# A ConvFFN in seven products per step: sums that grow in PSUM banks, and the low parts of weights on VectorE

## The chip, the cores and the metric

The kernel runs on one core of a Trainium2 chip. Its engines are TensorE (PE; PEld in the profile is its weight load), VectorE (DVE), ScalarE (ACT), GpSimd (POOL) and SyncE (SP), whose queue starts the DMA transfers spoken of here. The metric is the device time of one execution in microseconds, the median of several runs. Lower is better.

## The reference

Two layers act on 1024 latent tokens and 256 context tokens of width 1024, in float32. Layer 0 mixes tokens with a Fourier transform and a spatial gate, layer 1 with neighbourhood attention; each then has a ConvFFN, and this is what the change touches. Layer 0 runs it over latent and context tokens, layer 1 over the latent ones alone.

```
def conv_ffn(h, w_up, conv_w, conv_b, w_down):          # h: tokens x 1024, w_up: 1024 x 5632
    L = h.shape[1]
    a = h @ w_up
    gate, val = a[..., :D_FF], a[..., D_FF:]            # D_FF = 2816
    gp = jnp.pad(gate, ((0, 0), (CONV_W // 2, CONV_W // 2), (0, 0)))
    g = gp[:, 0:L] * conv_w[0] + gp[:, 1:1 + L] * conv_w[1] + gp[:, 2:2 + L] * conv_w[2] + conv_b
    return (jax.nn.silu(g) * val) @ w_down              # w_down: 2816 x 1024
    ...
    x = x + g2 * conv_ffn(modulate(x, norm2_g[layer], sh2, sc2), ffn_w_up[layer], ...)
```

## The kernel before

**Steps.** Features lie on partitions, tokens on columns. The tokens of a layer are worked in two halves, and each half runs 22 steps f = 0 to 21; a step makes the gate features and the value features of one block of 128. So a layer has 44 steps and the kernel 88. A step's product of a 1024 x 256 weight block (A) with the half's tokens (B) is cut into 2 x 2 blocks and made with seven products in place of eight (Strassen's scheme in Winograd's form): P1 = A00 B00, P2 = A01 B10, P3 = S4 B11, P4 = A11 N4, P5 = S1 T1, P6 = S2 T2, P7 = S3 T3. S1 to S4 are sums of weight blocks, T1 to N4 sums of token blocks. The columns of one product are 320 and 324 in layer 0's halves, 256 and 258 in layer 1's.

**Hi and low.** Every operand is split into a rounded part (hi) and the rest (low). `split` makes the hi as a copy on ScalarE (L447) and the low as a subtraction (L448) on VectorE or GpSimd. A product is then 4 blocks of rows x 3 passes (hi hi, hi low, low hi) = 12 matmuls (L306), 84 a step.

**Sums of a step.** ScalarE copies P1's bank into SBUF (L323). Seven VectorE adds (L311) bring in the six other products: c10 = P6 + c00, c00 += P2, c01 = P5 + c10, c10 += P7, c11 = c10 + P5, c10 += P4, c01 += P3. Then the gate: a scaled copy on ScalarE (L315), two shifted multiply-adds on VectorE for the convolution of width 3 (L317, L319), Silu on ScalarE, the product with the value half (L361), and a hi and a low of the result, `act`.

**Down.** `act` of two steps feeds `down` (L376): a step from f = 2 to 20 runs four of its output blocks (48 matmuls; 24 of 512 columns where a half has 512 tokens, layer 1's first). VectorE adds each result from PSUM into the running stream `xl` (L382). AFTER says behind which products the four stand. PSUM has eight banks under the name `pq`, taken in turn by products and `down`.

**Weights.** Each step also makes ready the operands of the next ones. Two DMAs of 512 KB on SP's queue (L236) bring the raw weights into `wr`: load0 brings A00 and A01, load1 brings A10 and A11. `wr` has two buffers, so load0 waits until the buffer that held the last A00 and A01 has been read, load1 until that of A10 and A11 has. GpSimd makes four raw sums: S1 = A10 + A11 (L241), S3 = A00 - A10 in A10's place (L247), S2 = S1 - A00 in A00's place (L248), S4 = A01 - S2 (L251). Seven splits follow. The seven hi and low pairs have one slot each: A00 and S2 side by side in one `wh` tile, S1 and S4 in another, A01, S3 and A11 in a `wq` tile each. The splits of a step are for the step after it, so a slot can be rewritten when this step's product has read it. The `down` weights come by a third DMA (`wrd`) and are split into `wd`.

**Who makes the lows.** With POOL = ("A00", "A01", "A11"), these three lows are made on GpSimd in steps that run `down`; the four others, those of `wd` and of `act` are VectorE's.

**What sets the order.** ORDER is the order of products from f = 1 on: P1, P2, P6, P5, P7, P4, P3. FEED says behind which product each piece of weight work is written. The written order is then rearranged by a scheduler that simulates the engines; the sums, the gate and the split of `act` have high priority. Every engine runs its own list in order, so an instruction that waits holds up all that stand behind it on that engine.

## Time and profile before

| | |
|---|---|
| median of 3 runs | 2914.47 us (2912.04 to 2919.38) |
| profiled execution | 2920.99 us, span 2919.1 us |
| PE busy | 2772.8 us, 95% |
| DVE busy | 2216.9 us, 76% |
| ACT busy | 1302.0 us, 45% |
| POOL busy | 1267.9 us, 43% |

Busy time is a sum over the span; the rest of an engine's time it waits. A group of instructions is shown by line, engine, operation, tiles (out<-in), shapes and count, then its busy time in us and the mean of one in ns, then the idle time of the engine just before them and what ended it. In a timeline a row is start, duration (both us), engine, line, operation, and in brackets the idle time before it. The rows themselves stand in the prediction.

### The profile page before, as it was taken

The numbers are of one execution on the slowest core, as the hardware profiler recorded it, in microseconds if no ns is written. First come the engines' busy times: TensorE is split into PE (matmuls) and PEld (weight loads), VectorE is DVE, ScalarE is ACT, GpSimd is POOL, SyncE is SP. The second block draws the span as 40 slices with busy tenths as digits, with TensorE's granted clock in tenths as the row PEclk, the third lists the DMA queues.
The fourth block names the chain that finished last, engine by engine and source line by source line (L and its number), as shares of the span: only waits on it lengthen the run. The fifth ranks groups of instructions, "written<-read, shape, count | busy, mean of one in ns | idle before, by whom it ended". The sixth has DMA issues, their size and how long they took to land.

```text
span 2919.1 us, 47590 instructions
## 1 busy us (share of the span) xinstructions
PE 2772.8 (95%) x17978; PEld 2522.4 (86%) x17978; DVE 2216.9 (76%) x3748; ACT 1302.0 (45%) x2448; POOL 1267.9 (43%) x1044
## 2 busy tenths in 40 slices
PE   7999998899999999999999998999989999899998
PEld 4668877799999899999888888998778888799998
DVE  4243477999989999998767668996498777887786
ACT  4221314434444443443443336996354444444443
POOL 0600025455555755553311112443455665666663
PEclk9999999899999999999899999999989999999999
DMA  8663262322223222222052327772133323333323
GB/s 303 215 189 118 98 217 72 112 74 86 80 87 101 75 80 87 73 81 87 24 169 101 137 109 183 180 179 80 37 109 101 95 87 98 105 89 93 94 88 95
DMA packets 335886, 327.67 MB, mean 112 GB/s; under 512 B 16217, under 2 KB 264617, under 8 KB 335657
## 3 DMA queue, kind: packets, MB, share of 16 engines
q1 hardware_dynamic: 331509, 315.69, 35.9%
q0 software_dynamic: 3808, 7.87, 0.9%
q8 instruction: 143, 2.34, 0.3%
q10 hardware_dynamic: 340, 1.06, 0.1%
q14 instruction: 86, 0.70, 0.1%
HBM read 277.86 MB, written 46.71 MB: 111 GB/s over the span
## 4 chain that ended last, share of the span: by engine, by line
PE 61%; DVE 14%; DMA 7%; POOL 7%; issue 5%; ACT 5%; SPq 0%; POOLq 0%; DVEq 0%; ACTq 0%
PE pq L306 18%; PE pq L478 15%; PE pq L376 11%; PE ps L478 6%; DMA wr<-in_ffn_w_up_dram 4%; POOL ws L241 2%; DVE xl L382 2%; DVE wh L448 2%; PE pq L566 2%; POOL wh L448 2%; DVE hx L311 2%; PE ps L487 2%; ACT t L1227 1%; POOL wr L248 1%; DMA wd<-in_ada_w_dram 1%
## 5 line engine op out<-in xcount | busy, mean ns | idle before, releaser
L376 PE MATMUL pq<-act,wd 128*128 128x320 f32 (+3 forms) x3696 | 639.8, 322 | 59.3 <-DVE xl L382 24.5
L376 PEld LDWEIGHTS pq<-act,wd 128*128 128x128 f32 x3696 | 557.1, 193 | 92.0 <-DVE xl L382 28.7
L306 PE MATMUL pq<-hs,wh 128*128 128x320 f32 (+3 forms) x4128 | 607.5, 299 | 16.3 <-DVE xl L382 7.8
L306 PEld LDWEIGHTS pq<-hs,wh 128*128 128x128 f32 x4128 | 576.9, 191 | 26.4 <-DVE xl L382 11.2
L306 PE MATMUL pq<-hs,wq 128*128 128x320 f32 (+3 forms) x3144 | 469.8, 299 | 8.4 <-DVE wq L448 4.9
L478 PE MATMUL pq<-hs,wh 128*128 128x512 f32 (+3 forms) x2100 | 469.0, 358 | 3.6 <-DVE hs L724 1.9
L306 PEld LDWEIGHTS pq<-hs,wq 128*128 128x128 f32 x3144 | 442.5, 191 | 14.1 <-DVE wq L448 5.7
L478 PEld LDWEIGHTS pq<-hs,wh 128*128 128x128 f32 x2100 | 365.8, 193 | 78.0 <-issue 6.2
L241 POOL TENSOR_TENSOR ws<-wr 128x512 f32<-128x512 f32 x88 | 153.6, 1745 | 397.3 <-DMA wr<-in_ffn_w_up_dram 333.0
L447 ACT ACTIVATE wh<-wr 128x512 fp32r<-128x512 f32 (+1 forms) x223 | 161.8, 726 | 354.0 <-POOL wr L248 201.5
L382 DVE SCALAR_TENSOR_TENSOR xl<-pq,mod,xl 128x320 f32<-128x320 f32 (+5 forms) x616 | 304.1, 514 | 11.7 <-PE pq L376 11.6
L448 DVE TENSOR_TENSOR wh<-wr,wh 128x512 fp32r<-128x512 f32 (+1 forms) x147 | 166.9, 1135 | 184.8 <-ACT wh L447 184.5
L448 POOL TENSOR_TENSOR wq<-wr,wq 128x512 fp32r<-128x512 f32 x152 | 235.7, 1550 | 32.9 <-ACT wq L447 32.9
L478 PE MATMUL ps<-hs,wh 128*128 128x512 f32 x840 | 240.0, 405 | 3.6 <-ACT hs L721 1.8
L311 DVE TENSOR_TENSOR hx<-hx,pq 128x320 f32<-128x320 f32 (+3 forms) x440 | 196.1, 448 | 29.1 <-PE pq L306 21.6
L447 ACT ACTIVATE wq<-wr 128x512 fp32r<-128x512 f32 x262 | 160.0, 623 | 101.3 <-PE pq L306 73.2
L447 ACT ACTIVATE wh<-ws 128x512 fp32r<-128x512 f32 x172 | 107.5, 625 | 169.8 <-PE pq L306 115.4
L478 PEld LDWEIGHTS ps<-hs,wh 128*128 128x128 f32 x840 | 141.9, 191 | 41.6 <-issue 14.4
L251 POOL TENSOR_TENSOR ws<-wr 128x512 f32<-128x512 f32 x88 | 120.2, 1366 | 123.3 <-DVE wh L448 112.3
L999 POOL TENSOR_TENSOR hsp<-hsq,hsp 128x512 fp32r<-128x512 f32 (+1 forms) x40 | 47.1, 1185 | 265.5 <-ACT hsq L998 265.5
L1006 DVE RECIPROCAL hsq<-hsq 128x512 f32<-128x512 f32 (+1 forms) x40 | 121.1, 3030 | 52.9 <-ACT hsq L1005 52.1
L448 DVE TENSOR_TENSOR wd<-wrd,wd 128x512 fp32r<-128x512 f32 x176 | 155.5, 912 | 0.2 <-ACT wd L447 0.2
(310 smaller groups left out, 4555.5 us busy)
## 6 DMA issues: line engine op xcount, KB each, us to landing
wr<-in_ffn_w_up_dram SPq DMA_DIRECT2D x176, 512.0 KB, 4.4
wrd<-in_ffn_w_down_dram SPq DMA_DIRECT2D x88, 512.0 KB, 3.5
adaw<-in_ada_w_dram SPq DMA_DIRECT2D x128, 256.0 KB, 3.6
wd<-in_ada_w_dram SPq DMA_DIRECT2D x32, 512.0 KB, 5.1
wr<-in_odd_w_qkv_dram SPq DMA_DIRECT2D x24, 512.0 KB, 3.9
vd<-kvs SPq DMA_DIRECT2D x8, 1280.0 KB
v<-vd SPq DMA_DIRECT2D x16, 640.0 KB
kd<-kvs SPq DMA_DIRECT2D x8, 1280.0 KB, 4.6
```

The source lines that it names most:

```text
L241: op(raw["S1"], raw["A10"], raw["A11"], ALU.add)
L251: op(x, raw["A01"], raw["S2"], ALU.subtract)
L306: nc.tensor.matmul(o, w[wn][:, wp, k], self.part(s, bn, k, sp), start=(k == 0 and i == 0), stop=(k == 3 and i == 2))
L311: nc.vector.tensor_tensor(o, x, y, ALU.add)
L376: nc.tensor.matmul(pd, self.wds[j][i][:, wp, d % 4], self.acts[f][:, sp, lo:lo + m], start=(i == 0 and pi == 0), stop=(i == len(fs) - 1 an ...
L382: nc.vector.scalar_tensor_tensor(x, pd[:, a - lo:b - lo], net.mod[:, self.layer, st, 5, d:d + 1], x, ALU.mult, ALU.add)
L447: self.nc.scalar.activation(h, src, AF.Copy)
L448: return (e or self.nc.vector).tensor_tensor(l, src, f32(h), ALU.subtract)
L478: nc.tensor.matmul(o, w(wp, k), s(k, sp), start=(ki == 0 and pi == 0), stop=(ki == len(order) - 1 and pi == 2))
L487: nc.tensor.matmul(out, l[a], r[b], start=(first and i == 0), stop=(last and i == 2))
L566: nc.tensor.matmul(acc[32 * q:32 * q + 32, 0:256], self.sT[:, k, :], w[q // 2][:, 256 * (q % 2):256 * (q % 2) + 256], start=(k == 0), stop ...
L1006: nc.vector.reciprocal(r, r)
```

## The change

For f = 0 nothing changes in the sums. For f > 0, P6 is accumulated in PSUM onto the bank that holds P1, P7 onto P6's, P3 onto P5's, and in steps f = 3 to 20 P4 onto P7's. After each link ScalarE copies the bank's state into SBUF, as far as it is needed there: c00 after P1, c01 after P6, c10 after P7, and c10 again after P4. The adds fall from seven to three (to four at f = 1, 2 and 21, where P4 keeps its own bank and add); the copies rise from one to four (to three). Summed over the four halves, 324 adds go and 240 copies come. A product that continues in a bank must wait until the copy has been read from it.

All lows are made on VectorE: the 228 of A00, A01 and A11 that GpSimd made move there. One `down` of a step stands behind P7 instead of P5. No line of the weight loads or raw sums is edited; their places in each engine's list move with the scheduler. (Lines L311 to L382 of before are L313 to L401 after; L447 and L448 are L466 and L467, L323 is L325.)

```diff
--- before.py
+++ after.py
@@ -92,14 +92,14 @@
 
     ORDER = ("P1", "P2", "P6", "P5", "P7", "P4", "P3")
     FEED = dict(P2=("A00",), P6=("A01",), P5=("S2",), P7=("S1", "load0"), P4=("S3", "A11", "load1"), P3=("S4", "s"))
-    AFTER = dict(P5=1, P4=1, P3=2)
+    AFTER = dict(P7=1, P4=1, P3=2)
     AFTER2 = dict(P4=1, P3=3)
 
     ORDER0 = ("P1", "P2", "P3", "P5", "P6", "P7", "P4")
     FEED0 = dict(P1=("A00",), P2=("A01",), P5=("S1",), P6=("S2", "load0"), P7=("S3",), P4=("A11", "load1", "S4", "s"))
     FEED1 = dict(P6=("A00", "A01"), P5=("S2",), P7=("S1", "load0"), P4=("S3", "A11", "load1"), P3=("S4", "s"))
     BESIDE = {1: (1, 3, 6), 2: (1, 2, 4, 5, 6), 3: (1, 2, 4, 5, 6)}
-    POOL = ("A00", "A01", "A11")
+    POOL = ()
 
     def __init__(self, net, layer, xs, slabs, pool):
         self.net, self.nc, self.layer, self.xs, self.slabs, self.pool = net, net.nc, layer, xs, slabs, pool
@@ -299,12 +299,14 @@
         g = self.t([P, self.w2], "g", bufs=1)[:, :2 * n]
 
         def product(p):
+
             wn, bn = self.PROD[p]
-            o = net.t(net.ps, [P, 512], "pq" if p in ("P2", "P5") else "pq")[:, :n]
+            o = net.t(net.ps, [P, 512], "pq")[:, :n] if p not in onto else x[onto[p]]
             for k in range(4):
                 for i, (wp, sp) in enumerate(PASSES):
-                    nc.tensor.matmul(o, w[wn][:, wp, k], self.part(s, bn, k, sp), start=(k == 0 and i == 0),
-                                     stop=(k == 3 and i == 2))
+                    nc.tensor.matmul(o, w[wn][:, wp, k], self.part(s, bn, k, sp),
+                                     start=(p not in onto and k == 0 and i == 0),
+                                     stop=(k == 3 and i == 2), skip_group_check=p in onto)
             return o
 
         def add(o, x, y):
@@ -319,16 +321,33 @@
                 nc.vector.scalar_tensor_tensor(g[:, c:c + m - 1], C0[:, c + 1:c + m], w2, g[:, c:c + m - 1],
                                                ALU.mult, ALU.add)
             nc.scalar.activation(g, g, AF.Silu)
-        x = {}
-        todo = [("P1", lambda: nc.scalar.activation(c00, x["P1"], AF.Copy)),
-                ("P1 P6", lambda: add(c10, x["P6"], c00)),
-                ("P6 P2", lambda: add(c00, c00, x["P2"])),
-                ("P6 P5", lambda: add(c01, x["P5"], c10)),
-                ("P6 P5 P7", lambda: add(c10, c10, x["P7"])),
-                ("P6 P5 P7", lambda: add(c11, c10, x["P5"])),
-                ("P6 P5 P7 P4", lambda: add(c10, c10, x["P4"])),
-                ("P6 P5 P3", lambda: add(c01, c01, x["P3"])),
-                ("P6 P5 P3 P2", gate)]
+        def copy(o, x):
+            nc.scalar.activation(o, x, AF.Copy)
+        x, onto = {}, {}
+        last = f > 2 and len(downs) > 0
+        if f == 0:
+            todo = [("P1", lambda: copy(c00, x["P1"])),
+                    ("P1 P6", lambda: add(c10, x["P6"], c00)),
+                    ("P6 P2", lambda: add(c00, c00, x["P2"])),
+                    ("P6 P5", lambda: add(c01, x["P5"], c10)),
+                    ("P6 P5 P7", lambda: add(c10, c10, x["P7"])),
+                    ("P6 P5 P7", lambda: add(c11, c10, x["P5"])),
+                    ("P6 P5 P7 P4", lambda: add(c10, c10, x["P4"])),
+                    ("P6 P5 P3", lambda: add(c01, c01, x["P3"])),
+                    ("P6 P5 P3 P2", gate)]
+        else:
+
+            onto = dict(P6="P1", P7="P6", P3="P5")
+            if last:
+                onto["P4"] = "P7"
+            todo = [("P1", lambda: copy(c00, x["P1"])),
+                    ("P2", lambda: add(c00, c00, x["P2"])),
+                    ("P6", lambda: copy(c01, x["P6"])),
+                    ("P7", lambda: copy(c10, x["P7"])),
+                    ("P7", lambda: add(c11, c10, x["P5"])),
+                    ("P4", lambda: copy(c10, x["P4"]) if last else add(c10, c10, x["P4"])),
+                    ("P3", lambda: add(c01, c01, x["P3"])),
+                    ("P3", gate)]
         order, feed = (self.ORDER if f else self.ORDER0, self.FEED if f >= 2 - s else (self.FEED0, self.FEED1)[f])
         cut = 3 - f if f < 2 and s == 0 else 7
         for i, p in enumerate(order):
```

**GpSimd, layer 0's first half, one step.** The tiles are `ws` and `wr` (raw), `wh` and `wq` (the hi and low pairs); the number behind a name is the buffer's. Before:

```order
L241 TENSOR_TENSOR ws_958_7242<-wr_952_7184 128x512
L247 TENSOR_TENSOR wr_952_7184<-wr_948_7147,wr_952_7184 128x512
L448 TENSOR_TENSOR wh_596_3834<-wr_948_7147,wh_596_3834 128x512
L448 TENSOR_TENSOR wq_589_3809<-wr_948_7147,wq_589_3809 128x512
L248 TENSOR_TENSOR wr_948_7147<-ws_958_7242,wr_948_7147 128x512
L251 TENSOR_TENSOR ws_958_7242<-wr_948_7147 128x512
L448 TENSOR_TENSOR wq_608_4158<-wr_952_7184,wq_608_4158 128x512
L241 TENSOR_TENSOR ws_982_7452<-wr_976_7394 128x512
```

And with the change:

```order
L241 TENSOR_TENSOR ws_944_7584<-wr_939_7527 128x512
L247 TENSOR_TENSOR wr_939_7527<-wr_936_7491,wr_939_7527 128x512
L248 TENSOR_TENSOR wr_936_7491<-ws_944_7584,wr_936_7491 128x512
L251 TENSOR_TENSOR ws_944_7584<-wr_936_7491 128x512
L241 TENSOR_TENSOR ws_964_7789<-wr_959_7732 128x512
```

The three lows (L448) are gone from between the raw sums; the four sums keep their order.

**ScalarE, layer 0's first half, an even step.** `g` is the gate (L323 here is its Silu), `hx` takes the copies. Before, from the copy of P1 (L323) over the hi of A01, `act`, S1, S2, S3 and A11 to that of S4:

```order
L323 ACTIVATE hx_840_6198<-pq_842_6200 128x320
L447 ACTIVATE wq_589_3809<-wr_828_6097 128x512
L447 ACTIVATE act_839_6194<-g_817_5989 128x640
L447 ACTIVATE wh_597_3835<-ws_838_6192 128x512
L447 ACTIVATE wh_596_3834<-wr_828_6097 128x512
L447 ACTIVATE wq_590_3810<-wr_832_6134 128x512
L447 ACTIVATE wq_608_4158<-wr_832_6134 128x512
L447 ACTIVATE wh_597_3835<-ws_838_6192 128x512
```

With the change:

```order
L466 ACTIVATE wq_589_3809<-wr_756_5646 128x512
L466 ACTIVATE wh_597_3835<-ws_764_5739 128x512
L323 ACTIVATE g_747_5541<-g_747_5541 128x640
L466 ACTIVATE wh_596_3834<-wr_756_5646 128x512
L325 ACTIVATE hx_766_5745<-pq_768_5747 128x320
L466 ACTIVATE act_765_5741<-g_747_5541 128x640
L466 ACTIVATE wq_590_3810<-wr_759_5682 128x512
L325 ACTIVATE hx_766_5745<-pq_768_5747 128x320
```

These begin with A01, S1, the Silu and S2 (`wh` from `wr`). Behind S2 now stands the copy of P6 (the first L325), and behind the hi of `act` and S3 that of P7, both from bank `pq_768`, which held P1 before and will hold P4.

**ScalarE, layer 1's first half.** Before, over the end of a step, where `wr_3222` holds A10 (then S3) and A11, `wr_3219` A00 (then S2), and `wr_3239` the next A00:

```order
L447 ACTIVATE wh_3041_20746<-wr_3219_22436 128x512
L447 ACTIVATE wh_3042_20747<-ws_3226_22502 128x512
L447 ACTIVATE wq_3025_20649<-wr_3222_22464 128x512
L447 ACTIVATE wq_3048_20973<-wr_3222_22464 128x512
L447 ACTIVATE wh_3042_20747<-ws_3226_22502 128x512
L315 ACTIVATE g_3229_22509<-hx_3228_22508,cols1_31_139,cols4_175_786 128x512
L447 ACTIVATE wd_3253_22726<-wrd_3235_22560 128x512
L447 ACTIVATE wd_3254_22729<-wrd_3235_22560 128x512
L447 ACTIVATE wh_3041_20746<-wr_3239_22608 128x512
```

With the change, where `wr_2999` holds A11 and `wr_3013` the next A00:

```order
L466 ACTIVATE wd_3024_22145<-wrd_3010_21984 128x512
L466 ACTIVATE wd_3025_22148<-wrd_3010_21984 128x512
L466 ACTIVATE wh_2879_20542<-wr_3013_22029 128x512
L325 ACTIVATE hx_3020_22099<-pq_3022_22101 128x256
L466 ACTIVATE wq_2886_20769<-wr_2999_21889 128x512
L325 ACTIVATE hx_3004_21932<-pq_3006_21934 128x256
L466 ACTIVATE wh_2880_20543<-ws_3002_21926 128x512
L317 ACTIVATE g_3005_21933<-hx_3004_21932,cols1_31_139,cols4_175_786 128x512
```

The hi of A11 (`wq` from `wr_2999`) stood before the next load's A00; it now stands behind it (`wh` from `wr_3013`).

## The prediction

> **What bounds the kernel now.** I read the page's busy line and its slices first, then a table of four stretches that hold the steady ConvFFN steps (layer 0 first and second half, layer 1 first and second half), then the chain of waits, then single steps.
>
> ```profile
> PE 2772.8 (95%) x17978; PEld 2522.4 (86%) x17978; DVE 2216.9 (76%) x3748; ACT 1302.0 (45%) x2448; POOL 1267.9 (43%) x1044
> ```
>
> TensorE is busy for 95% of 2919.1 us, so at most 146 us are to be had, wherever they lie.
>
> ```profile
> core 0: us, PE busy (x) PEld busy (x) DVE busy (x) ACT busy (x) POOL busy (x), PEclk, DMA share, GB/s
> 639.00:911.00 272.00, 272.00 (x1852) 271.83 (x1851) 248.54 (x435) 112.82 (x183) 152.40 (x98) 1.00 0.27 82
> 1030.70:1366.30 335.60, 335.22 (x2247) 332.69 (x2246) 305.75 (x532) 137.99 (x223) 183.10 (x119) 1.00 0.27 81
> 2151.20:2500.00 348.80, 324.93 (x2149) 296.68 (x2149) 278.51 (x437) 155.87 (x277) 211.17 (x145) 0.97 0.33 98
> 2594.50:2879.00 284.50, 263.54 (x2114) 261.06 (x2113) 215.03 (x403) 117.97 (x210) 182.20 (x112) 0.98 0.30 89
> ```
>
> GpSimd runs seven weight operations a step, so 98, 119 and 112 operations are 14, 17 and 16 steps: 272.0/14 = 19.43 us a step, 335.6/17 = 19.74, and 284.5/16 = 17.78 in the last stretch. In layer 0 PE is busy throughout; in layer 1 it stands still for 24 and 21 us. What PE alone needs is in the chain of waits (start, us, engine, tile, line, count):
>
> ```profile
> 254.57 5.57 PE ps L478 x24
> 642.48 7.05 PE pq L306 x48
> 1030.71 7.14 PE pq L306 x48
> 2204.84 5.69 PE pq L306 x48
> 2752.82 5.79 PE pq L306 x48
> ```
>
> A matmul takes 7.05/48 = 146.9 ns (320 columns), 148.8 (324), 118.5 (256), 120.6 (258), 232 (512). A step has 84 matmuls of products and 48 of `down` (24 of 512 columns in layer 1's first half): 132 x 146.9 = 19.39, 132 x 148.8 = 19.64, 84 x 118.5 + 24 x 232 = 15.52, 132 x 120.6 = 15.92. So layer 0 is bound by PE to 0.1 us a step, whatever VectorE does. Layer 1 is bound by something else; its period in the first half is read from the load at the head of each step:
>
> ```profile
> 2410.41 4.83 DMA wr<-in_ffn_w_up_dram
> 2427.54 4.83 DMA wr<-in_ffn_w_up_dram
> ...
> 2478.28 4.75 DMA wr<-in_ffn_w_up_dram
> ```
>
> Four steps from 2410.41 to 2478.28: 16.97 us each. What bounds there is in GpSimd's timeline of a step of the second half (start, us, last bracket the idle time before it and who ended it):
>
> ```profile
> 2650.28 2.88 POOL L241 TENSOR_TENSOR ws<-wr 128x512 f32<-128x512 f32 x1 [5.67 <-DVE g L319]
> 2653.24 1.63 POOL L247 TENSOR_TENSOR wr<-wr,wr 128x512 f32<-128x512 f32 x1
> 2654.83 1.73 POOL L448 TENSOR_TENSOR wh<-wr,wh 128x512 fp32r<-128x512 f32 x1
> 2656.53 1.28 POOL L448 TENSOR_TENSOR wq<-wr,wq 128x512 fp32r<-128x512 f32 x1
> 2657.77 1.28 POOL L248 TENSOR_TENSOR wr<-ws,wr 128x512 f32<-128x512 f32 x1
> 2659.13 1.27 POOL L251 TENSOR_TENSOR ws<-wr 128x512 f32<-128x512 f32 x1
> 2660.84 1.29 POOL L448 TENSOR_TENSOR wq<-wr,wq 128x512 fp32r<-128x512 f32 x1 [0.44 <-ACT wq L447]
> 2668.02 3.10 POOL L241 TENSOR_TENSOR ws<-wr 128x512 f32<-128x512 f32 x1 [5.90 <-DMA wr<-in_ffn_w_up_dram]
> ```
>
> It is a closed loop: seven operations, then the second load of raw weights, which may start only when the A11 low (the last L448) has read its buffer, and 17.74 us later the next L241. In it the S2 hi comes late, and VectorE, which runs in order, waits for it:
>
> ```profile
> 2659.75 1.20 DVE L448 TENSOR_TENSOR wh<-wr,wh 128x512 fp32r<-128x512 f32 x1 [4.33 <-ACT wh L447]
> 2661.40 3.15 PE L376 MATMUL pq<-act,wd 128*128 128x258 f32 x24 [1.95 <-DVE xl L382]
> ```
>
> Behind that S2 low stand the `xl` adds that empty PSUM, and PE stops 1.95 us for a bank.
>
> **The change part by part.** *Adds and copies.* 324 adds go (none at f=0, three a step at f=1, 2, 21, four in the 18 others, in four halves) and 240 copies on ScalarE come (two or three a step).
>
> ```profile
> L311 DVE TENSOR_TENSOR hx<-hx,pq 128x258 f32<-128x258 f32 x80 | 33.1, 414 | 1.1
> L323 ACT ACTIVATE hx<-pq 128x258 f32<-128x258 f32 x16 | 5.8, 365 | 0.0
> L448 DVE TENSOR_TENSOR wq<-wr,wq 128x512 fp32r<-128x512 f32 x16 | 11.2, 702 | 0.0
> L447 ACT ACTIVATE wq<-wr 128x512 fp32r<-128x512 f32 x48 | 28.0, 616 | 0.0
> ```
>
> By these rows of the same window of layer 1's second half, a steady step loses 4 x 0.41 = 1.66 us of VectorE and gains 3 x 0.70 = 2.11 of it for the lows, and 3 x 0.365 = 1.10 on ScalarE. Layer 1's VectorE goes from 215.0/16 = 13.4 us a step to about 13.9, under PE's 15.9, and layer 0's from 17.8 to some 18, under 19.4: neither engine sets an end by its total. PE's count does not change; that one `down` stands behind P7, not P5, only enters the counts of matmuls below. So the 324 adds are worth nothing in themselves; PE covers them.
>
> *A wait is added.* P6 may not write P1's bank before ScalarE's copy has left it, P7 not before P6's copy, P4 not before P7's. Nothing in this trace continues a bank after a copy, so bounds: nothing where ScalarE is free (P2's 12 matmuls, 12 x 120.6 = 1.45 us, cover a copy of 0.365), up to a whole hi and a copy where ScalarE stands in its order before another instruction.
>
> *Lows off GpSimd, layer 1's second half.* Out of the loop go 1.73 and 1.28, and the A11 low falls from 1.29 to 0.70. Then the loop is shorter than PE's step. What is left: P4 of an odd step frees A11's slot, and before the next step's first `down` with the newest `act` come A11 hi 0.62, low 0.70, the load 4.15 (alone, quoted below) to 4.83, L241 1.35 (its value in layer 0, below; the 2.88 here is read beside VectorE's two-input operations), S1 hi 0.62, and behind it on ScalarE the hi of that `act`, about as long: 8.06 to 8.74. One engine's next instruction follows 0.08 us after (2653.16 to 2653.24 above); I take 0.1 for each of seven handovers: 8.8 to 9.4. PE has 75 matmuls there (counted in its new order), 75 x 120.6 = 9.05 us. So 0 to 0.4 us of stall every second step, and PE's own 15.92; with a little `xl` waiting left I take 16.3. (17.78 - 16.3) x 18 = 27 us gained; bounds 33 (15.92 and nothing) and 19 (16.7).
>
> *Layer 1's first half.* In the order of the changed kernel ScalarE takes the hi of the next A00, which waits for the first load, before the hi of A11, which frees the buffer of the second. The two loads, side by side before, then stand one behind the other in one loop: L241 1.35 to 1.42, L247 1.53 to 1.63, L248 1.28, S2 hi 0.62 and low 1.20, load 4.15, A00 hi 0.62, copy 0.365, A11 hi 0.62 and low 0.70, load 4.15 to 4.83: 16.6 to 17.4, some handovers lying in the loads' times already.
>
> ```profile
> 521.64 4.15 DMA wr<-in_ffn_w_up_dram
> 2415.37 1.42 POOL L241 TENSOR_TENSOR ws<-wr 128x512 f32<-128x512 f32 x1 [4.99 <-DMA wr<-in_ffn_w_up_dram]
> ```
>
> Against 16.97 now: nothing, give or take 0.3 a step, 5 us in 18. The stall of the old loop goes, and the serial loads take its place.
>
> *Layer 0.* PE leaves nothing to gain, so only a loss is possible. GpSimd's seven become four, the DMAs stay (on SP some loads stand a place earlier or later):
>
> ```profile
> L248 POOL TENSOR_TENSOR wr<-ws,wr 128x512 f32<-128x512 f32 x14 | 24.5, 1750 | 0.0
> L247 POOL TENSOR_TENSOR wr<-wr,wr 128x512 f32<-128x512 f32 x14 | 21.4, 1528 | 1.1
> L241 POOL TENSOR_TENSOR ws<-wr 128x512 f32<-128x512 f32 x14 | 18.8, 1345 | 62.1 <-DMA wr<-in_ffn_w_up_dram 44.9 <-DVE g L317 17.2
> L447 ACT ACTIVATE wq<-wr 128x512 fp32r<-128x512 f32 x42 | 26.4, 629 | 24.0 <-PE pq L306 23.9
> L323 ACT ACTIVATE hx<-pq 128x320 f32<-128x320 f32 x14 | 5.8, 417 | 0.0
> 733.17 1.29 POOL L448 TENSOR_TENSOR wq<-wr,wq 128x512 fp32r<-128x512 f32 x1 [1.06 <-ACT wq L447]
> ...
> 739.19 1.47 POOL L241 TENSOR_TENSOR ws<-wr 128x512 f32<-128x512 f32 x1 [4.74 <-DMA wr<-in_ffn_w_up_dram]
> ```
>
> In its new order ScalarE has the S2 hi (for the next step) ahead of the copy of P6, and P7 waits for that copy. From the end of P4 in an odd step: A11 hi 0.63, low 0.70, load and issue 4.73 (733.17 + 1.29 to 739.19), L241 1.35, L247 1.53, L248 1.28 (as in layer 1's second half) to 1.75, S2 hi 0.63, copy 0.42: 11.3 to 11.7, with up to four handovers 11.4 to 12.1. PE has 71 matmuls between that P4 and P7, 71 x 146.9 = 10.43. So P7 is 1.0 to 1.7 us late in 9 even steps: 12 us lost. In odd steps PE has 101 matmuls there, 14.84 us: no loss. In the second half of layer 0 it has 78 x 148.8 = 11.6: 0 to 0.5 in 9 steps, 2 us lost.
>
> *First steps.* Around 520 to 600 us VectorE itself is full:
>
> ```profile
> 520.00:600.00 80.00, 71.98 (x448) 68.80 (x447) 76.95 (x126) 37.82 (x66) 37.97 (x25) 0.96 0.37 108
> ```
>
> PE idles 8 us beside 96% of VectorE. Only in step 1 of each half do adds go and no low comes (GpSimd took lows only once `down` runs): 3 x 0.48 (layer 0's L311) x 4 = 5.8 us, if VectorE sets the pace; I take half, 3 us gained, bounds 0 and 5.8.
>
> **Sum.** -27 + 0 + 12 + 2 - 3 = -16 us. The profiled execution took 2920.99 us (span 2919.1 and 1.9 around it), 6.5 over the median; 2905 by it, and 2914.47 - 16, about 2898, by the median.
>
> **The rivals.** *PE bounds both layers (0.13).* If ScalarE is early enough everywhere, layer 0 loses nothing and layer 1's first half falls to 15.52 too: 1.45 x 18 = 26, with 33 for the second half and 3 at the start: -62, 2852. For it: VectorE and ScalarE have room. Against: ScalarE's order is fixed, and has the next A00 before A11.
>
> *GpSimd stays slow (slower, 0.18).* L241 takes 2.9 us in layer 1's second half and 1.35 elsewhere; VectorE now runs 0.5 us more of two-input operations a step beside it. If the four raw sums cost the middle of both, 2.1, wherever a chain above has L241 in it, 0.8 us more goes to each: layer 0 loses 19 + 9, layer 1's first half 14, the second half gains 19, the start 3: +20, 2934. It decides from a mean of L241 of about 1.8 us. For it: the row of 2.88 stands beside L448 on VectorE. Against: in layer 0 VectorE is busier, 248.54/14 = 17.8 us a step, and L241 takes 1345 ns.
>
> The Trainium skill, page SBUF — State Buffer, section Who interferes with whom, says that a VectorE operation with two inputs in SBUF and a reading GpSimd operation exclude each other entirely. Fully blocked, the S2 low at 2659.75 would have taken about 0.70 + 0.65, the rest of the L251 beside it, 1.35; it took 1.20, so this trace is near the rule. By it the three lows cost the raw sums as much as before, and the rival above is the one it favours.
>
> *Gains and losses cancel (0.19).* Layer 1's second half at 16.7 (19 gained), its first half at its bad bound (5 lost), layer 0 and the start as summed: -19 + 5 + 14 - 3 = -3, 2911; with nothing gained at the start 2914.
>
> **How the numbers follow.** Forecast 0.50: 2898, its own range 2885 to 2911. This kernel's runs tell about 0.3%, 9 us, from no change, so faster is below 2906, slower above 2923. The forecast puts some 0.39 below 2906, the rest in between with the cancelling case; with the first rival 0.52 faster, 0.27 same, 0.21 slower. Eight in ten: from inside the first rival, 2862, to the slower one, 2934.
>
> **What would show it.** Layer 1's second half at 16.0 to 16.5 us a step, and no PE wait of 2 us on `xl` there. Layer 1's first half still near 17.0, with the two loads end to end. In layer 0, every second step, PE idle of 1 to 1.7 us before P7, ended by ScalarE's copy; PE busy 272.0 of 272.0 there would refute it. L241 near 1.35 in all four stretches; at 2 us or more the second rival holds. Wrong altogether, if layer 0's steps grow by more than 2 us or shrink at all.

## The result: slower by 2.6%, where a small gain was forecast

The changed kernel takes 2989.02 us (median of 4 runs, 2987.93 to 2994.47) against 2914.39 us for the kernel before: a ratio of 1.0258, 95% interval 1.0239 to 1.0276. It is 75 us slower, where 16 us faster was forecast, and far above the forecast's own range of 2885 to 2911. The profiled execution has a span of 2986.1 us, 67.0 more than before.

The page's busy line of the changed kernel:

```profile
PE 2792.4 (94%) x17978; PEld 2532.2 (85%) x17978; DVE 2277.7 (76%) x3652; ACT 1378.4 (46%) x2688; POOL 905.9 (30%) x816
```

The counts say that the change does what it says: 240 more instructions on ScalarE (2448 to 2688), 228 fewer on GpSimd (1044 to 816), 96 fewer on VectorE (324 adds less, 228 lows more). No engine is fuller than before by a share that matters. PE's idle time grew by 47.4 us (146.3 to 193.7). Its busy time for the same 17978 matmuls grew by the other 19.6, at a granted clock of 0.970 over the whole execution in place of 0.974; why, was not looked into. Most of the loss is waiting, as PE's groups of the `down` and product matmuls show (the last fields are PE's idle time before them and what ended it):

```profile
L395 PE MATMUL pq<-act,wd 128*128 128x320 f32 (+3 forms) x3696 | 636.4, 322 | 84.7 <-ACT act L466 55.3 <-DVE act L467 25.1 <-DVE hx L313 2.5
L307 PE MATMUL pq<-hs,wh 128*128 128x320 f32 (+3 forms) x4128 | 621.0, 300 | 16.5 <-DVE hx L313 4.2 <-ACT hx L325 4.0 <-ACT hs L466 3.4
L307 PE MATMUL pq<-hs,wq 128*128 128x320 f32 (+3 forms) x3144 | 483.1, 301 | 35.0 <-ACT hx L325 29.8 <-ACT wq L466 2.1 <-DVE hs L467 1.4
```

PE waits 80 us for `act` (55.3 for its hi, 25.1 for its low) and 34 us for copies out of linked banks (L325). The same groups of the kernel before:

```profile
L376 PE MATMUL pq<-act,wd 128*128 128x320 f32 (+3 forms) x3696 | 639.8, 322 | 59.3 <-DVE xl L382 24.5 <-ACT act L447 21.0 <-DVE hx L311 10.0
L306 PE MATMUL pq<-hs,wh 128*128 128x320 f32 (+3 forms) x4128 | 607.5, 299 | 16.3 <-DVE xl L382 7.8 <-ACT wh L447 4.9 <-DVE wh L448 2.6
```

There `act` stood for 21.0 us by its hi (and 2.6 by its low), the `xl` adds for 32.3, and copies of a linked bank did not exist.

Where in the program: the table takes the start of the hi of `act` (once a step) as the mark. It compares the profiled executions of before, of the change, and of four experiments told below, in us.

| stretch | before | changed | lows alone | down behind P5 | P4's own bank | S hi on GpSimd |
|---|---|---|---|---|---|---|
| layer 0, first half, f = 3 to 20 | 328.8 | 343.9 | 323.6 | 344.6 | 335.6 | 336.5 |
| layer 0, second half | 332.9 | 345.0 | 330.8 | 344.5 | 339.3 | 338.9 |
| layer 1, first half | 286.9 | 305.8 | 279.8 | 303.6 | 276.8 | 296.7 |
| layer 1, second half | 297.5 | 294.8 | 290.5 | 291.6 | 287.4 | 289.9 |
| f = 0 to 3, four halves | 196.3 | 216.4 | 205.6 | 213.5 | 212.3 | 209.5 |
| f = 20 to 21, four halves | 73.1 | 78.3 | 68.6 | 78.3 | 69.5 | 74.8 |

From before to changed: +15.1, +12.1, +18.9, -2.7, +20.1 and +5.2, together 68.7, of 67.0 in the span. A mark moves against PE's work from kernel to kernel: between the same two marks stand, by kernel, up to some 90 matmuls more or less, and 7 matmuls are about 1 us. So a row can tell 10 us too much or too little. PE's idle time between the marks does not count that work:

| PE idle in | before | changed | lows alone |
|---|---|---|---|
| layer 0, first half, f = 3 to 20 | 2.2 | 13.7 | 0.0 |
| layer 0, second half | 0.4 | 10.5 | 0.0 |
| layer 1, first half | 15.8 | 28.1 | 12.9 |
| layer 1, second half | 21.6 | 19.6 | 12.2 |
| f = 0 to 3, four halves | 21.8 | 29.2 | 19.5 |
| f = 20 to 21, four halves | 8.0 | 19.7 | 8.3 |

Windows of the same lengths in the changed kernel, which begin some 10 us behind the marks of the four steady stretches (span, then busy time of PE, PEld, DVE, ACT and POOL with counts, granted clock, DMA share, GB/s):

```profile
595.90:939.80 343.90, 331.36 (x2243) 328.73 (x2242) 314.83 (x511) 153.67 (x277) 105.18 (x71) 1.00 0.27 81
1065.00:1410.00 345.00, 334.50 (x2219) 330.54 (x2218) 296.83 (x500) 148.14 (x264) 98.64 (x64) 1.00 0.25 77
2245.30:2551.10 305.80, 277.25 (x1804) 248.59 (x1803) 245.09 (x341) 137.59 (x273) 104.46 (x71) 0.98 0.30 92
2662.60:2957.40 294.80, 275.93 (x2223) 271.11 (x2222) 257.16 (x397) 137.82 (x262) 96.12 (x64) 0.99 0.29 86
```

In layer 0, where PE was busy throughout, it now stands still for 12.5 and 10.5 us in these windows. The granted clock is 1.00 there, so this is no throttle.

How one such wait is made shows in the chain of waits around 1210 us, layer 0's second half:

```profile
1208.55 0.64 ACT wq L466
...
1209.94 4.42 DMA wr<-in_ffn_w_up_dram
...
1214.49 1.32 POOL ws L241
...
1219.44 0.65 ACT wh L466
...
1220.11 0.87 DVE wh L467
1220.98 0.75 issue
1221.72 0.83 DVE act L467
```

PE's P4 ends, then come the hi of A11 and (left out here) its low, the second load, the first raw sum and two more, the hi and low of S2, and only behind them the low of `act`, for which `down` waits at the end (PE idles 0.52 us here): 14 us from 1208.55 to 1222.55. The low of `act` needs nothing of the load. It stands behind the low of S2 in VectorE's list, which took 1.69 us in this step beside a raw sum on GpSimd, and 0.69 undisturbed. The hi of `act` is not held up here: it begins at 1220.14, and the product of its gate ended at 1220.10. Over the steps f = 3 to 20 that gap is some 0.1 us or less in the mean in layer 0, and 1.1 and 1.0 us in the halves of layer 1, where in about every second step the hi waits 1.7 to 3.1 us behind that of S1 on ScalarE. Before, it was 0.03 to 0.05 everywhere.

### The profile page after: what moved, and what is told of

The parts are those of the page before. It is cut to its first block, busy times and chain, and to the rows that moved or that the text cites. A ratio compares the mean times of both kernels' runs of the same rounds, so it can differ in the third digit from the quotient of the medians.

```text
span 2986.1 us, 47226 instructions
## 1 busy us (share of the span) xinstructions
PE 2792.4 (94%) x17978; PEld 2532.2 (85%) x17978; DVE 2277.7 (76%) x3652; ACT 1378.4 (46%) x2688; POOL 905.9 (30%) x816
## 4 chain that ended last, share of the span: by engine, by line
PE 51%; DVE 17%; DMA 13%; ACT 9%; POOL 5%; issue 5%; SPq 0%; POOLq 0%; ACTq 0%; DVEq 0%
PE pq L307 15%; PE pq L497 14%; DMA wr<-in_ffn_w_up_dram 10%; PE pq L395 10%; PE ps L497 6%; ACT t L1246 3%; DVE wh L467 3%; DVE wq L467 2%; POOL ws L241 2%; DVE act L467 2%; PE pq L585 2%; DVE xl L401 2%; PE ps L506 2%; ACT wh L466 1%; DVE hs L467 1%
## 5 line engine op out<-in xcount | busy, mean ns | idle before, releaser
L395 PE MATMUL pq<-act,wd 128*128 128x320 f32 (+3 forms) x3696 | 636.4, 322 | 84.7 <-ACT act L466 55.3
L307 PE MATMUL pq<-hs,wh 128*128 128x320 f32 (+3 forms) x4128 | 621.0, 300 | 16.5 <-DVE hx L313 4.2
L307 PE MATMUL pq<-hs,wq 128*128 128x320 f32 (+3 forms) x3144 | 483.1, 301 | 35.0 <-ACT hx L325 29.8
L241 POOL TENSOR_TENSOR ws<-wr 128x512 f32<-128x512 f32 x88 | 131.7, 1497 | 936.0 <-DMA wr<-in_ffn_w_up_dram 692.8
L401 DVE SCALAR_TENSOR_TENSOR xl<-pq,mod,xl 128x320 f32<-128x320 f32 (+5 forms) x616 | 297.4, 511 | 28.2 <-PE pq L395 27.8
L466 ACT ACTIVATE wh<-wr 128x512 fp32r<-128x512 f32 (+1 forms) x223 | 161.9, 726 | 281.0 <-DMA wr<-in_ffn_w_up_dram 75.8
L467 DVE TENSOR_TENSOR wh<-wr,wh 128x512 fp32r<-128x512 f32 (+1 forms) x223 | 212.9, 955 | 93.0 <-ACT wh L466 91.5
L466 ACT ACTIVATE wq<-wr 128x512 fp32r<-128x512 f32 x262 | 163.8, 626 | 252.3 <-PE pq L307 221.0
L467 DVE TENSOR_TENSOR wq<-wr,wq 128x512 fp32r<-128x512 f32 x262 | 227.9, 870 | 44.2 <-ACT wq L466 42.4
L467 DVE TENSOR_TENSOR wh<-ws,wh 128x512 fp32r<-128x512 f32 x172 | 156.8, 912 | 73.4 <-ACT wh L466 69.4
L466 ACT ACTIVATE wh<-ws 128x512 fp32r<-128x512 f32 x172 | 108.3, 629 | 195.1 <-POOL ws L241 132.2
L251 POOL TENSOR_TENSOR ws<-wr 128x512 f32<-128x512 f32 x88 | 134.4, 1527 | 69.4 <-DVE wh L467 60.6
L248 POOL TENSOR_TENSOR wr<-ws,wr 128x512 f32<-128x512 f32 x88 | 137.6, 1564 | 33.4 <-DVE wh L467 28.4
L313 DVE TENSOR_TENSOR hx<-hx,pq 128x320 f32<-128x320 f32 (+3 forms) x284 | 126.3, 447 | 26.4 <-PE pq L307 24.3
```

What stands on the lines that cost most here:

```text
L241: op(raw["S1"], raw["A10"], raw["A11"], ALU.add)
L248: op(x, raw["S1"], x, ALU.subtract)
L251: op(x, raw["A01"], raw["S2"], ALU.subtract)
L307: nc.tensor.matmul(o, w[wn][:, wp, k], self.part(s, bn, k, sp), start=(p not in onto and k == 0 and i == 0), stop=(k == 3 and i == 2), ski ...
L313: nc.vector.tensor_tensor(o, x, y, ALU.add)
L395: nc.tensor.matmul(pd, self.wds[j][i][:, wp, d % 4], self.acts[f][:, sp, lo:lo + m], start=(i == 0 and pi == 0), stop=(i == len(fs) - 1 an ...
```

## The experiments

**Which part of the change?** Four kernels: the sums alone, the lows alone, the changed kernel with its `down` behind P5 again, and the kernel before with that `down` behind P7.

The sums alone:

```diff
-    POOL = ()
+    POOL = ("A00", "A01", "A11")
```

> The sums grow in PSUM and the `down` stands behind P7 as in the change, but the lows of A00, A01 and A11 stay on GpSimd. Theory 1 (the new copies: P7 waits for the copy of P6, which stands on ScalarE behind weight splits that wait for the load and the raw sums; the place of the lows matters little): 2970 to 2995, with the idle time of PE ended by the copies (L325) about the 33 us of the changed kernel. Theory 2 (the lows: on VectorE they stand in line with the low of `act`, and `act` comes late): 2905 to 2925, with no more than 10 us of PE idle ended by `act`. If both are needed, 2930 to 2960.

Measured: 3006.41 us, ratio 1.0291 (1.0260 to 1.0323), somewhat beyond what theory 1 gave. PE waits 86.6 us for `act` and 37.3 for copies. The sums alone make all of the loss.

The lows alone (the kernel before with one edit):

```diff
-    POOL = ("A00", "A01", "A11")
+    POOL = ()
```

> The kernel before with all lows on VectorE, and nothing else. Theory 1 (copies): 2890 to 2915, since GpSimd's chain gets shorter and no copy is added; layer 1's second half at 16.0 to 16.7 us a step. Theory 2 (lows): 2960 to 2990, with PE idle of 40 us or more ended by `act`. If both are needed: 2920 to 2950.

Measured: 2894.34 us, ratio 0.9927 (0.9903 to 0.9951): 21 us faster, within what theory 1 gave except that layer 1's second half only comes to 17.1 us a step. PE waits 25.0 us for `act`. Theory 2 falls. GpSimd's work on lows was worth taking away.

```diff
-    AFTER = dict(P7=1, P4=1, P3=2)
+    AFTER = dict(P5=1, P4=1, P3=2)
```

> The changed kernel with the one `down` back behind P5. Theory 1 and 2 both: within 10 us of the changed kernel's 2989, as the `down` only moves between two products. Rival (the place of the `down` takes cover from the copy of P6): 2940 to 2965, or worse than 3000 if less stands between P6 and P7.

Measured: 2978.84 us, ratio 1.0214 (1.0195 to 1.0233), 10 to 13 us better than the changed kernel: at the edge of what the theories gave, and far from the rival's. And the same edit the other way round in the kernel before:

```diff
-    AFTER = dict(P5=1, P4=1, P3=2)
+    AFTER = dict(P7=1, P4=1, P3=2)
```

> The kernel before with the one `down` behind P7 in place of P5, and nothing else. Theories 1 and 2: within 9 us of 2914. Rival (the place of the `down` by itself makes `act` late or the odd and even steps unequal): 2930 or more.

Measured: 2923.31 us, ratio 1.0022 (1.0010 to 1.0034). The place of that `down` is a small matter on both sides. In summary, from 2914 to 2989: the lows -21 (2894), the sums +85 (2979, `down` behind P5), the `down` behind P7 +10.

**What in the sums?** The loss shows as PE waiting for `act` far more than for copies, so theory 1 in its first form (copies) does not hold alone. Counted in the order of instructions, from the product that ends a gate to the first `down` that reads its `act` (steps where that is nearest), before has 79, 79, 72 and 83 matmuls in the four halves, lows alone 79, 79, 75 and 88, and the changed kernel 72, 61 to 69, 62 to 76 and 64: `down` comes sooner. In layer 0's first half the compiled order of a step was P1, P2, P6, P5, `down`, P7, P4, `down`, P3, `down`; with the links it is P1, P2, P5, `down`, P6, `down`, P7, `down`, P4, P3, with almost only `down` between P6, P7 and P4. Theory A says that this is the loss, theory B the copies, theory C the loop of loads in layer 1.

With `down` one step further behind (the final steps take over what is left; the lines that move the rest by one step are left out):

```diff
-                ups.append(self.up(s, f, hooks, [lambda d=d, j=f - 2: self.down(s, j, j % 2 * 4 + d) for d in range(4)]
-                                   if 2 <= f < NF - 1 else [], lambda f=f: prep(f),
+                ups.append(self.up(s, f, hooks, [lambda d=d, j=f - 3: self.down(s, j, j % 2 * 4 + d) for d in range(4)]
+                                   if 3 <= f else [], lambda f=f: prep(f - 1),
...
```

> The changed kernel, with each step's `down` working on pairs of `act` one step older, so that 119 to 180 matmuls stand between the product that ends a gate and the first `down` that reads its `act`, where 61 to 76 stood. Theory A (the accumulation costs its time because the scheduler puts `down` into the gaps between the linked products, earlier than `act` is there): the 80 us of PE idle ended by `act` fall below 25, and the time to 2905 to 2930. Theory B (the waits for copies between linked products are the cost): idle ended by `act` falls but that ended by the copies (36 us) grows in its place; 2960 to 2990. Theory C (layer 1 is held by the loop of loads): layer 0 at 19.4 to 19.8 us a step, layer 1 still 17 to 18, total 2940 to 2960.

Measured: 2920.06 us, ratio 1.0013 (1.0004 to 1.0023). PE's groups:

```profile
L307 PE MATMUL pq<-hs,wh 128*128 128x320 f32 (+3 forms) x4128 | 625.2, 301 | 55.3 <-DVE hx L313 22.0 <-ACT wh L469 15.3 <-DVE wh L470 12.6
L395 PE MATMUL pq<-act,wd 128*128 128x320 f32 (+3 forms) x3696 | 607.5, 316 | 6.9 <-ACT act L469 3.9 <-DVE xl L401 1.8 <-DVE xc L401 0.8
L307 PE MATMUL pq<-hs,wq 128*128 128x320 f32 (+3 forms) x3144 | 476.9, 299 | 24.8 <-ACT hx L325 18.7 <-ACT wq L469 2.8 <-DVE wq L470 1.4
```

The wait for `act` falls from 80 to 3.9 us and that for copies from 34 to 21.9 in all, so B's shift does not occur. Some 43 us come up elsewhere, as waits for VectorE's adds (22.0, from 4.2) and for the splits in `wh` (27.9, from 3.0). Layer 0 is at 19.4 and 19.5 us a step and layer 1 at 17.1 and 16.8, so A holds for the larger part and C for the rest.

> The kernel before with all lows on VectorE and the same one step older `act`. Theory A: the 25 us of PE idle ended by `act` go, 2865 to 2880. Theory C: layer 1 stays at its 16.5 to 17.4 us a step, 2880 to 2894. Theory B says nothing on it (no links).

The same edit with the sums as before: 2895.22 us, ratio 0.9935 (0.9916 to 0.9954), no different from lows alone and just above both ranges. PE's wait for `act` does go, from 25.0 to 1.5 us, but others take its place (for the `xl` adds 27.8 in place of 9.3), so theory A's gain does not come without the links. The first half of layer 1 falls to 15.7 us a step by the marks, but that is work moved: its window has some 80 matmuls fewer, and the steps at the halves' ends have 130 more (83.6 us against 68.6).

In layer 1, with two more raw buffers, so that no load waits for the A11 low of its own turn (layer 0 keeps its two):

```diff
-            t = net.t(net.wpool, [P, KD, P], "wr", bufs=2)
+            own = i == 1 and self.layer == 1
+            t = net.t(self.pool if own else net.wpool, [P, KD, P], "wrx" if own else "wr", bufs=2)
```

> The changed kernel, where in layer 1 the loads of A10 and A11 have two buffers of their own (four raw buffers in place of two), so that no load waits for the A11 low of the same turn. Theory C: layer 1's halves fall from 18.0 and 17.3 to 15.8 to 16.6 us a step, 2935 to 2960; layer 0 unchanged. Theory A: `act` still comes late by its own chain on ScalarE and VectorE, layer 1 not below 17.0, 2970 to 2989.

Measured: 2938.74 us, ratio 1.0079 (1.0064 to 1.0094): 50 us better. Layer 1 is at 16.1 and 16.8 us a step, layer 0 unchanged at 20.2. So the load held layer 1 in good part. The late `act` is cured only in part with it: in layer 1's steady steps PE's wait for `act` falls from 38 to 23 us, that for copies from 11 to under 1.

With P4 in a bank of its own and the `down` behind P5:

```diff
-        last = f > 2 and len(downs) > 0
+        last = False
```

> The changed kernel with P4 in a bank of its own and an add (as it has at f = 1, 2 and 21) in all steps, and the `down` behind P5: the chain of links is one shorter. Theory B: the idle time of PE ended by copies halves to some 18 us, 2950 to 2965. Theory A: the first `down` on a new `act` stands 61 to 86 matmuls behind, hardly later than in the changed kernel, so 2965 to 2985.

Measured: 2923.88 us, ratio 1.0028 (1.0017 to 1.0039), 54 us better by the ratios than the same kernel with P4 linked (1.0214). Neither theory gave as much. PE's groups of this kernel:

```profile
L395 PE MATMUL pq<-act,wd 128*128 128x320 f32 (+3 forms) x3696 | 638.6, 320 | 47.6 <-ACT act L466 32.8 <-DVE act L467 10.8 <-ACT wd L466 1.2
L307 PE MATMUL pq<-hs,wq 128*128 128x320 f32 (+3 forms) x3144 | 479.7, 300 | 25.9 <-ACT hx L325 20.6 <-DVE wq L467 2.7 <-DVE hs L467 1.4
```

The product matmuls' wait for copies is 21.5 us where it was 33.2, that for `act` 43.6 where it was 75.1. In the order, P4 with its own bank stands before P7 in most steady steps, in layer 0's first half up to 8 `down` matmuls behind P6; linked, it comes behind P7 and the `down` between, with only P3 after it. Its A11 slot, and so the raw buffer and the second load, come free that much sooner.

**Is it the place of P4 alone?** With the sums as before and only this link (P7 is first added into c11, so that its bank may grow):

```diff
+        if f > 2 and len(downs) > 0:
+            onto = dict(P4="P7")
...
-                ("P6 P5 P7", lambda: add(c10, c10, x["P7"])),
-                ("P6 P5 P7", lambda: add(c11, c10, x["P5"])),
+                ("P6 P5 P7", lambda: add(c11, c10, x["P7"]) if onto else add(c10, c10, x["P7"])),
+                ("P6 P5 P7", lambda: add(c11, c11 if onto else c10, x["P5"])),
```

> All lows on VectorE and the sums of the kernel before, but with one link: P4 is accumulated onto P7's bank (f = 3 to 20), P7 having been added into c11 first; as many adds as before and no new copy. Theory D (it is the place of P4: linked to P7 it comes late in the step, so the A11 slot, its raw buffer, the second load and what follows it come late): 2915 to 2950, slower than the 2894 of all lows on VectorE. Theory E (P4's link costs only because it closes a chain of copies on ScalarE): 2885 to 2905, since here P4 waits for one add and no copy.

Measured: 2906.12 us, ratio 0.9958 (0.9942 to 0.9975), against 0.9927 for lows alone: some 9 us, at the edge of what can be told, and 1 us above theory E's range. PE waits 51.9 us for adds in place of 15.2, 30 of them in layer 1's steady steps, which are no longer for it. Layer 0's are (19.8 and 20.0 us against 19.0 and 19.5), and there GpSimd's first raw sum (L241) takes 3.8 to 3.9 us in the mean in place of 1.4, which this run does not separate from the link. P4 is the last product of a step here, so theory D falls: its late place costs little where no copy hangs on it. The 54 us are not the place of P4 alone.

The lists of ScalarE show what else differs. With the sums as before, in all four halves the hi of `act` stands before those of S2 (`wh` from `wr`) and S1 (`wh` from `ws`); here lows alone, layer 0:

```
L447 ACTIVATE act_863_6404<-g_841_6199 128x640
L447 ACTIVATE wh_596_3834<-wr_852_6307 128x512
L447 ACTIVATE wh_597_3835<-ws_862_6402 128x512
```

In the changed kernel S1 stands ahead of `act`, and in every second step of layer 0 S2 does too, in the first half with the copy of P6:

```
L466 ACTIVATE wh_597_3835<-ws_804_6149 128x512
L323 ACTIVATE g_787_5951<-g_787_5951 128x640
L466 ACTIVATE wh_596_3834<-wr_796_6056 128x512
L325 ACTIVATE hx_806_6155<-pq_808_6157 128x320
L466 ACTIVATE act_805_6151<-g_787_5951 128x640
```

S1 and S2 wait for the second load and for raw sums. Theory F says that this is what ties `act` and the copies to the load. To take the two hi parts off ScalarE, GpSimd makes them:

```diff
+            if self.busy and name in ("S1", "S2"):
+                nc.gpsimd.tensor_copy(h, x)
+                nc.vector.tensor_tensor(l, x, f32(h), ALU.subtract)
```

> The changed kernel with the `down` behind P5 (2979), where in steps with `down` the hi of S1 and of S2 is copied on GpSimd in place of ScalarE, so that on ScalarE the copies and the hi of `act` no longer stand behind instructions that wait for the second load and the raw sums. Theory F (ScalarE's list is what ties `act` and the copies to the load): idle of PE ended by copies and by `act` together falls from 109 us below 60, 2900 to 2945. Theory G (the place of P4 at the end of the step and the early `down` do it by themselves): 2965 to 3000.

Measured: 2939.64 us, ratio 1.0077 (1.0057 to 1.0096), 40 us better than the same kernel with these two on ScalarE, and inside theory F's range. Its groups:

```profile
L400 PE MATMUL pq<-act,wd 128*128 128x320 f32 (+3 forms) x3696 | 636.1, 321 | 54.5 <-ACT act L471 42.8 <-DVE xl L406 4.7 <-DVE act L472 4.4
L312 PE MATMUL pq<-hs,wq 128*128 128x320 f32 (+3 forms) x3144 | 482.4, 300 | 26.6 <-ACT hx L330 19.1 <-DVE wq L472 2.7 <-ACT hs L471 1.4
```

The wait for the low of `act` is nearly gone (26.1 to 4.4), that for copies down from 33.7 to 21.0, that for its hi only from 49.0 to 42.8: 68 us together, not below 60 as F had it. In layer 0's first half the copies' 12.9 us are gone, and in layer 1 the hi of `act` no longer stands waiting behind its gate (0.2 us or less in the mean, from 1.2 and 0.8). What stays of the wait for the hi fits the early `down` (60 to 72 matmuls behind the product in this kernel), which this run leaves. Theory G falls.

**Which kernel is best, and what do the links cost when all else is cured?** Four runs with the four raw buffers in layer 1: with the sums as before, with the links but P4's own bank, with the sums as before and `down` a step further behind, and with all links and that `down`.

> All lows on VectorE, sums as before, and in layer 1 two raw buffers of its own for A10 and A11 (four in place of two). If the loop through the load holds layer 1: its steps fall from 16.5 and 17.1 to 15.6 to 16.2 us, 2860 to 2880. If `act` or the raw sums hold it: 2885 to 2897.

Measured: 2856.64 us, ratio 0.9790 (0.9776 to 0.9805), a little below the first range. Layer 1 is at 15.2 and 15.8 us a step, and PE idles 1.5 and 0.0 us there in place of 12.9 and 12.2: the loop through the load was its hold.

> The changed kernel with P4 in a bank of its own, the `down` behind P5, and the four raw buffers in layer 1. What the links P1-P6, P7 and P5-P3 cost by themselves, against the run above with the sums as before and the same buffers: 10 to 20 us if they cost only in layer 0, where P7 waits for the copy of P6 (2880 to 2900); 30 us or more if they cost in layer 1 too (2900 to 2915).

Measured: 2912.44 us, ratio 0.9980 (0.9968 to 0.9992). Three links cost 56 us here, as the second expectation had it (30 us or more, 2900 to 2915): by the marks 21 of them in layer 0's steady steps and 30 in layer 1's (16.1 and 16.6 us a step against 15.2 and 15.8), of which 8 and 14 show as idle time of PE. With these buffers P4's own bank wins 26 us (2939 to 2912, some 10 of it by the place of the `down`), where it won 54 with two: P4's link works for a good part through layer 1's loop of loads.

> As the run with four raw buffers and the sums as before, with `down` on pairs of `act` one step older as well. If the load loop was layer 1's only hold: no difference to it beyond 9 us. If `act` is the next hold: 2845 to 2865 with layer 1 at 15.4 to 16.0 us a step.

Measured: 2848.31 us, ratio 0.9762 (0.9747 to 0.9776): 8 us less, inside the 9 of the first case, so no next hold can be told. It is the best of all kernels here, 2.4% faster than before and 4.8% faster than the changed one. It keeps of the change the lows on VectorE and nothing of the sums.

> The changed kernel with the `down` behind P5, with `down` on `act` one step older, and with the four raw buffers in layer 1. With the sums as before these two cures gave 2848. If the copies still cost where ScalarE's list ties them to the load, in layer 0: 2870 to 2900, with 15 to 25 us of PE idle ended by copies. If early `act` and the loop were all: 2845 to 2860.

Measured: 2872.90 us, ratio 0.9845 (0.9823 to 0.9866). With all links, but late `act` and the load both cured, the links still cost 24 us. PE waits 16.2 us for copies, as foreseen, but only 3 of them in layer 0's steady steps.

Side by side, in us (the place of the one `down` is given, which is worth some 10):

| | sums as before | with the links | the links cost |
|---|---|---|---|
| all lows on VectorE | 2894 | 2979 (P5), 2989 (P7) | 85, 95 |
| and `act` one step older | 2895 | 2920 (P7) | 25 |
| and four raw buffers in layer 1 | 2857 | 2939 (P7) | 82 |
| and both | 2848 | 2873 (P5) | 25 |

The older `act` takes away some 60 to 70 us of what the links cost, with two raw buffers as with four. The buffers win 38 to 50 us with the links or without them, and take little off their cost.

## Why the prediction was wrong

The step that failed is "A wait is added". The prediction costed the copies, with their bounds, and gave the links no other price. By the runs the links cost 85 us (2979 against 2894), and a copy that has not yet left its bank is the smaller part. Some 60 to 70 us go when `down` takes `act` of one step earlier (the table that ends the experiments), so the larger part is `act` that comes later than the `down` drawn nearer to it. The prediction summed no chain to the low of `act`, though `down` waits for it. Three changes of the order lead there: almost only `down` can stand between P6, P7 and P4, so it comes sooner; P4 behind P7 frees the A11 slot late; and S1 and S2, which wait for the load, stand on ScalarE ahead of the hi of `act` (it is late by this in layer 1) and ahead of the copy of P6 (layer 0's first half). To undo one wins 54 (P4's own bank) or 40 us (S hi elsewhere), with waits for both `act` and copies falling each time; these gains overlap, and what each change costs by itself stays open.

*Layer 0's first half: right.* Predicted 12 us lost because the copy of P6 stands behind the hi of S2; measured +15.1 by the marks and +11.5 by PE's idle time. This row of the stretch from 595.9 to 939.8 shows 12.0 as PE's wait for copies, all before the matmuls on `wq`, in 8 waits of 1.5 us in the mean where 9 of 1.0 to 1.7 were summed, so the mechanism was right and not only the number:

```profile
L307 PE MATMUL pq<-hs,wq 128*128 128x320 f32 x612 | 98.7, 310 | 12.0 <-ACT hx L325 12.0
```

*Layer 0's second half: too small.* Predicted 2, measured +12.1. The chain was followed to the copy of P6 and compared with 78 matmuls. PE's 10.2 us of waiting stand before `down` instead, 8.1 for the hi of `act` and 2.1 for its low. In the step shown above the chain went on over the S2 low to the low of `act`, 14 us in all. The hi begins right behind its gate in this half; it is the gate that ends too late for a `down` that stands nearer than before, and why was not followed further.

*Layer 1's first half: wrong.* Predicted nothing, measured +18.9. The loop of two serial loads is there, as foreseen, but takes longer. One turn of it (first and next start of the first load):

```profile
2401.21 3.68 DMA wr<-in_ffn_w_up_dram
...
2407.15 3.87 DMA wr<-in_ffn_w_up_dram
...
2411.16 1.80 POOL ws L241
...
2414.78 1.76 DVE act L467
...
2418.17 0.69 DVE wh L467
...
2418.91 4.89 DMA wr<-in_ffn_w_up_dram
```

That is 17.70 us where 16.6 to 17.4 was summed. The two loads of the turn were below their price. From the start of L241 to the end of the S2 low the sum had 1.35 to 1.42, 1.53 to 1.63, 1.28, 0.62 and 1.20, about 6.1; it took 7.70. The S2 low waited 1.5 us for VectorE, which was on the lows of `act` and of a `wd` (1.76 and 1.78 us beside raw sums on GpSimd, where 0.69 is the undisturbed time); the sum left both out. The mean step is 18.0 us, and why it is longer than this turn was not followed. PE waits 18.4 us for `act` and 11.1 for copies in this half, where the sum had neither.

*Layer 1's second half: wrong.* Predicted -27, measured -2.7. The change's own row for P4 to the first `down`:

```profile
2746.23 0.10 ACT wh L466
...
2746.77 0.37 ACT hx L325
2747.14 0.53 ACT wq L466
...
2747.69 0.69 DVE wq L467
...
2748.41 5.22 DMA wr<-in_ffn_w_up_dram
...
2753.78 1.29 POOL ws L241
...
2755.75 0.58 DVE wh L467
...
2756.87 1.77 DVE act L467
```

From 2746.15 to 2758.68 it is 12.5 us, where 8.8 to 9.4 was summed against 9.05 of PE. Left out were the S1 low and the low of `act` (2755.75 to 2758.64, 2.9 us). By the timeline they took 1.20 and 1.75 us, again beside raw sums; the mean low of `act` in this half is 1.6 us, from 1.0 before. The load was 5.22, not at most 4.83. The copy and the A00 hi ahead of A11 made the rest.

*Lows off GpSimd: the gain is there, but alone.* Lows alone won 21 us where 27 was set for layer 1's second half. PE's idle time there fell by 9.4, and by 2.2, 0.4 and 2.9 us in the three other steady stretches; its busy time over the whole kernel fell too (2772.8 to 2764.3 us, at a granted clock of 0.978 in place of 0.974). With the links the second half kept 2 of the 9.4.

*First steps: wrong sign.* Predicted -3, measured +20 by the marks. The windows hold some 70 matmuls more, about 10 us, and PE's idle time grew by 7.4; with the lows alone it fell by 2.3. So the links cost there too, by what was not tried. The steps at the halves' ends had no term, and PE's idle time grew by 11.7 there.

*That the adds are worth nothing in themselves* agrees: with the sums alone there are 324 adds fewer, and no stretch is shorter than before.

*The rivals.* "PE bounds both layers" did not occur. "GpSimd stays slow" came nearest in time (2934) for another reason than its own: it decided from a mean of L241 of 1.8 us, and that fell from 1.7 to 1.5.

```profile
L241 POOL TENSOR_TENSOR ws<-wr 128x512 f32<-128x512 f32 x88 | 131.7, 1497 | 936.0 <-DMA wr<-in_ffn_w_up_dram 692.8 <-DVE wh L467 71.6 <-DVE xc L401 63.3
```

Not one of the cases had `act` as what becomes late. Of the signs that were named, PE's waits before P7 in layer 0 were seen, and layer 1's second half (17.3 us a step, not 16.0 to 16.5) and first half (18.0, not 17.0) were not. Layer 0's steps grew by 0.7 to 0.9 us, under the 2 us named for "wrong altogether", so that bound was too wide to tell.

## What to carry to other kernels

Sums in PSUM turn products that could run in any order into a chain; before linking them, count what independent matmuls are left to put between, and ask when the inputs of these are ready. A chain must be summed to the instruction that the waiting engine needs, through every in-order list on the way, and not only to the first wait that one has in mind; the work that stands behind a late instruction on ScalarE or VectorE is late with it, though it needs nothing of it. Where a load's buffer closes a loop, another buffer can be worth more than faster work inside the loop: here 40 us on top of the 21 of moving the lows. To tell whether a cure belongs to a change, run it without the change as well: the buffers won as much without the links, and the older `act` won nothing without them.

## What the runs showed of the hardware

The same raw sum on GpSimd (128 x 512, two inputs) took from 1.29 to 4.71 us in one kernel, that with the lows alone. In layer 1's second half, its mean, and one of its instances:

```profile
L241 POOL TENSOR_TENSOR ws<-wr 128x512 f32<-128x512 f32 x16 | 59.1, 3691 | 107.9 <-DMA wr<-in_ffn_w_up_dram 80.3 <-DVE wd L448 15.0 <-DVE xl L382 12.6
2767.44 4.71 POOL L241 TENSOR_TENSOR ws<-wr 128x512 f32<-128x512 f32 x1 [6.08 <-DVE xl L382]
```

VectorE beside that instance, which ends at 2772.15:

```profile
2767.91 1.29 DVE L448 TENSOR_TENSOR wd<-wrd,wd 128x512 fp32r<-128x512 f32 x2
2769.11 0.69 DVE L448 TENSOR_TENSOR wh<-wr,wh 128x512 fp32r<-128x512 f32 x1
2769.71 0.69 DVE L361 TENSOR_TENSOR g<-g,hx 128x516 f32<-128x516 f32 x1
2770.32 0.69 DVE L448 TENSOR_TENSOR wq<-wr,wq 128x512 fp32r<-128x512 f32 x1
2770.92 0.43 DVE L311 TENSOR_TENSOR hx<-pq,hx 128x258 f32<-128x258 f32 x1
2771.26 1.45 DVE L448 TENSOR_TENSOR act<-g,act 128x516 fp32r<-128x516 f32 x1
```

In the first four rows VectorE's operations keep their time (0.69 us each, 1.29 for two), and the sum waits. These rows read two tensors in SBUF; the fifth reads one of its two from PSUM, and from its start 2770.92 the 1.29 us of an undisturbed sum lead to 2772.21, about where this one ends. Then it is VectorE that waits: the low of `act` takes 1.45 us and ends at 2772.71, 0.56 behind the sum. That agrees with the Trainium skill, page SBUF — State Buffer, section Who interferes with whom, by which a VectorE operation with two SBUF inputs and a reading GpSimd operation exclude each other entirely, and one with a single SBUF input does not contend. It can also explain why lows alone gained 7 to 9 us in this stretch and not 27: 3.69 us of L241 stand in the loop where 1.35 was set. With four raw buffers the same sum is released by the low of S4 and no longer by the load, and runs at another point of the step:

```profile
L242 POOL TENSOR_TENSOR ws<-wrx 128x512 f32<-128x512 f32 x16 | 20.7, 1294 | 60.6 <-DVE wh L449 60.6
```

So part of what the buffers won may be this, 1.29 in place of 3.69 us in the loop; no run separates it from the earlier load. The changed kernel has 1.6 us there, with as many lows on VectorE. Its VectorE pays instead: the mean low of `act` in that half is 1.6 us, and 0.7 in the kernel with four raw buffers and the sums as before. Why the wait falls to one engine here and to the other there was not tried.
